# A two-layer decoder trunk: the first norm's sums with tokens on partitions, and a turn counter set to zero before attention

## The chip, the cores and the metric

The kernel runs on one core of one Trainium2 chip. The metric is the device time of one execution in microseconds (us). Three runs of the kernel before took 1446.49, 1443.2 and 1445.98 us; the median is 1445.98 us.

## The reference, cut to what matters

Two layers are computed on 512 tokens with 1024 features, all in float32. Cut to the lines around the change:

```
def rmsnorm(x, w):
    xf = xf * lax.rsqrt(jnp.mean(xf * xf, axis=-1, keepdims=True) + EPS)
    return xf.astype(x.dtype) * w

mod = c_act @ w_ada + b_ada            # sh1, sc1, g1, sh2, sc2, g2
h = rmsnorm(x, norm1_w) * (1 + sc1) + sh1
u = h @ w_in                           # pool, conv, q, k, v, gates
... three mixers; each is projected, gated by a sigmoid, and summed ...
x = x + g1 * (merged @ w_out)
h2 = rmsnorm(x, norm2_w) * (1 + sc2) + sh2
x = x + g2 * ((silu(h2 @ w_gate) * (h2 @ w_up)) @ w_down)
```

For each token the first norm needs one number, the reciprocal root of the mean square over 1024 features. The kernel holds `x` with features on the 128 partitions, as 8 tiles `x[k]` of 128 features by 512 tokens. The sum over features therefore crosses partitions, and that is done by TensorE.

## The kernel before

**Products.** Every float32 operand is split into a high and a low part of a format that TensorE reads in one pass, and a product is three matmuls (`mm3`, line 163): high by high, high by low, low by high. Weights arrive by DMA as `raw` tiles; ScalarE (ACT) makes `whi` (line 399) and VectorE (DVE) makes `wlo` (line 402). For some tiles in the projection `w_in` of layer 0, ACT makes both `whi` and the negated copy (lines 419 and 421) and a transfer that adds, issued by GpSimd's queue, finishes `wlo` (line 423). There are 3 `raw` buffers, and 5 each of `whi` and `wlo`.

**Order.** The program is written out for all engines by Python code. `matmul`, `transpose` and `pin` fix an instruction's place on its engine in program order; the rest is placed on ACT, DVE and the queues by a scheduling layer of the framework. Each engine works its own list strictly in order. Waits between engines are counts of semaphores; the framework derives them from what reads and writes which tile. In a built program `Activation_49`, `DVE_49` and `PE_49` are the counts of finished instructions of those engines.

**PSUM.** TensorE's outputs lie in 4 single tiles `mm` and 2 tiles `pair` of two banks each. One `pair` tile, `scratch` (line 872; `pair_126` in the orders below), holds the statistics of the opening in `scratch[:, 0]` and the warm-up's output in `scratch[:, 1]`. In the first stage of layer 0 it is used again: `pair_b = scratch` (line 941), and `pair_b[:, 0]` is the fourth of the four accumulators of the queries, `q_ps[3]`.

**The opening, lines 872 to 934.**
- Nine small matmuls of ones warm TensorE up, and 8 transposes spread the activated condition `c` over the partitions for ACT to copy into `csil`.
- As the tiles `x[k]` land, DVE and ACT square them (lines 894 and 899) and DVE adds them in pairs (line 901). Four matmuls of ones by such a pair add up over partitions in `scratch[:, 0]` (line 902), so that all partitions hold the sums of all 512 tokens.
- Nineteen matmuls of ones (line 906) keep TensorE busy meanwhile.
- ACT takes the reciprocal root (line 908) and its scaled square (line 909), and DVE does one Newton step in two instructions (lines 913 and 914), all on 128x512 elements, into `norm.rstd`.
- `ada_first` (line 499) makes one column of the scale SC1 or of the shift SH1 by a dot product on DVE (line 479) and one small ACT instruction (line 503 or 506).
- `first_scaled(k)` (line 654, DVE at line 657) multiplies `x[k]`, the scale and `rstd`. `first_hi(k)` (ACT, line 661) and `first_lo(k)` (DVE, line 664) then split the normed tile; ACT line 666 keeps it whole.

**The first stage of layer 0, lines 945 to 972.** For k = 0 to 7 the code writes the scale, shift, `first_scaled`, `first_hi` and `first_lo` of tile k + 2 ahead of the matmuls of tile k. Tiles 0 and 1 are written in the opening. For each k the matmuls are: three for each of `q_ps[0]` to `q_ps[3]`, then three for each of three feature tiles. Afterwards ACT copies the queries out of PSUM (lines 711 and 716, called from line 979) and the next features begin in the tile that `q_ps[0]` held.

**Turns.** `mm3` adds the columns of its output to `clock[0]` (line 168); at every 2048 columns `tick` (line 139) lets the attention's generators take a step, which writes their transposes and score products between the matmuls of the gates. The count runs on from stage to stage. Layer 0's attention begins with it at 0, and layer 1's at 1024, because the pooled projection (line 1198) adds two products of 512 in each layer.

Of the kernel before, what the change touches and what calls it, by code (L numbers as in the profile page):

```python
# [12 lines left out]
F32 = mybir.dt.float32  # L13
# [3 lines left out]
AF = mybir.ActivationFunctionType  # L17
ALU = mybir.AluOpType
# [3 lines left out]
P = 128  # L22
D = 1024
S = 512
L = 2
KT = D // P
# [3 lines left out]
TT = S // P  # L30
# [8 lines left out]
EPS = 1e-6  # L39
# [34 lines left out]

WARM = 9

WARM2 = 19

GATE2 = ([("gate", j) for j in range(6)] + [("attn", 0), ("attn", 1), ("gate", 6), ("gate", 7)]
         + [("attn", j) for j in range(2, 8)])  # L80
# [3 lines left out]
def hybrid_trunk(ctx, tc, xT, ws, ada, cols, pool_w, qk_w, crow, pos, con, out):  # L84
    nc = tc.nc
    V, A, T = nc.vector, nc.scalar, nc.tensor
# [10 lines left out]
    def nm(s):  # L97
        uid[0] += 1
        return f"{s}{uid[0]}"

    def bigt(dt=F32R):
        return big.tile([P, S], dt, tag="big", name=nm("big"))
# [4 lines left out]
    def ps_mm():  # L107
        return psum.tile([P, S], F32, tag="mm", name=nm("mm"), bufs=4)

    def ps_pair():  # L110
        return psum.tile([P, 2, S], F32, tag="pair", name=nm("pair"), bufs=2)
# [4 lines left out]
    def sm(shape, dt=F32, tag="sm", bufs=8):  # L116
        return small.tile(shape, dt, tag=tag, name=nm(tag), bufs=bufs)
# [5 lines left out]
    clock = [0, 0]  # L123
# [30 lines left out]
    def matmul(*a, **k):  # L154
        tc.keep_in_program_order(T.matmul(*a, **k))  # L155

    def pin(ins):
        return tc.keep_in_program_order(ins)

    def transpose(*a):  # L160
        tc.keep_in_program_order(T.transpose(*a))  # L161
# [40 lines left out]
    ident = const.tile([P, P], F32, name="ident")  # L202
# [3 lines left out]
    ones = f32(ones_r)  # L206
# [5 lines left out]
    epst = const.tile([P, 1], F32, name="epst")  # L212
# [32 lines left out]
    class Sums:  # L245
        def __init__(self, l, m, j):
            self.l, self.m, self.j = l, m, j
# [181 lines left out]
    split_after, last_hi = [None], [None]  # L429
# [47 lines left out]
    def ada_dot(aw, l, part, j):  # L477

        return V.scalar_tensor_tensor(aw, aw, 1.0, csil, op0=ALU.mult, op1=ALU.mult,  # L479
                                      accum_out=mod[l][:, part, j:j + 1])  # L480
# [4 lines left out]
    def ada_first_load(j, after=None, parts=(SC1, SH1)):  # L485
        tiles = {}
        for part in parts:
            tiles[part] = w4([P, D])
            with issued_after(after):
                nc.sync.dma_start(tiles[part], ada[0, part, j])  # L490
        return tiles
# [7 lines left out]
    def ada_first(j, tiles, part):  # L499
        first_dots[j, part] = pin(ada_dot(tiles[part], 0, part, j))  # L500
        m = mod[0][:, part, j:j + 1]
        if part == SC1:
            ins = A.activation(amod[0][0][:, j:j + 1], m, AF.Identity, scale=minus[:, j:j + 1],
                               bias=abias[:, j:j + 1])
        else:
            ins = A.activation(m, m, AF.Identity, bias=colt[:, 0, C_ADA + part * KT + j:C_ADA + part * KT + j + 1])
        if j == 0:

            pin(ins)
# [69 lines left out]


    class Norm:
        def __init__(self, one=False):
            self.one = one
            self.low = []
            self.acc = bigt(F32)
            self.last = bigt(F32)
            self.sums = [(bigt(), bigt()) for _ in range(1 if one else 2)]
            self.rstd = bigt(F32)
            self.hi = [bigt() for _ in range(KT)]
            self.lo = [bigt() for _ in range(KT)]  # L590
            self.h = [bigt(F32) for _ in range(KT)]
# [145 lines left out]
    def to_features(l, qk, which, hp):  # L737
        pt = ps_mm()
        for t in range(TT):
            transpose(pt[:, t * P:(t + 1) * P],  # L740
                      qk[t][:, which, 2 * hp:2 * hp + 2, :].rearrange("p h d -> p (h d)"), ident)
        return split_from(pt, scale=colt[:, l, C_QK + which:C_QK + which + 1])
# [110 lines left out]
    def start(gen):  # L853
        n = next(gen, None)
        if n is not None:
            fibers.append([n, gen])

    def attention(l, qk, v, nrq, prq, y_attn):

        for hp in range(PAIRS):  # L860
            q = to_features(l, qk, 0, hp)
            yield 1
            k = to_features(l, qk, 1, hp)
            y = bigt(), bigt()
            y_attn.append(y)
            yield 2
            for n, i in enumerate(ORDER):
                start(unit(hp, i, q, k, v, y, nrq, prq))
                yield GAP[n]


    scratch = ps_pair()
    norm = Norm()

    rows = [ps_mm(), ps_mm()]
    for i in range(WARM):
# [4 lines left out]
        if i == 6:  # L881
            for j in range(KT):
# [6 lines left out]
    pin(V.scalar_tensor_tensor(abias, colt[:, 0, C_ADA + SC1 * KT:C_ADA + (SC1 + 1) * KT], 1.0,  # L889
                               minus, op0=ALU.add, op1=ALU.mult))  # L890
    sq = [bigt(F32) for _ in range(KT)]
    for k in range(KT):
        if k == 0 or (k % 2 == 1 and k < KT - 1):
            step.append(pin(V.tensor_mul(sq[k], x[k], x[k])))
        else:
            if k in (2, 4):
                h = k // 2 - 1
                pin(A.activation(csil[:, h * S:(h + 1) * S], rows[h], AF.Copy))
            pin(A.activation(sq[k], x[k], AF.Square))
        if k % 2 == 1:  # L900
            step.append(pin(V.tensor_add(sq[k], sq[k - 1], sq[k])))
            matmul(scratch[:, 0], ones, sq[k], start=(k == 1), stop=(k == KT - 1))
    first[0].update(ada_first_load(0, step[3], (SH1,)))
    idle = ps_mm()
    for _ in range(WARM2):
        matmul(idle[:, :P], ones, ones, start=True, stop=True)
    y, y2, t = bigt(F32), bigt(F32), bigt(F32)
    A.activation(y, scratch[:, 0], AF.Abs_reciprocal_sqrt, bias=epst, scale=1.0 / D)
    split_after[0] = A.activation(y2, y, AF.Square, scale=(0.5 / D) ** 0.5)
    ada_first(0, first[0], SC1)  # L910
    ada_first(0, first[0], SH1)

    pin(V.scalar_tensor_tensor(t, scratch[:, 0], D * EPS, y2, op0=ALU.add, op1=ALU.mult))
    pin(V.scalar_tensor_tensor(norm.rstd, t, 1.5, y, op0=ALU.subtract, op1=ALU.mult))
    norm.first_scaled(0)
    norm.first_hi(0)
    fetch_after[0] = step[4]
# [19 lines left out]
    for l in range(L):  # L937
# [38 lines left out]
        ss = sm([P, TT, 2, HEADS], tag="ssq", bufs=1)  # L976
# [204 lines left out]
            return sg  # L1181

        m01, y_attn = [], []
        fibers.append([5, attention(l, qk, v, nrq, prq, y_attn)])
        bulk.append((0.4, pool_weights))
        for j in range(2):
# [45 lines left out]
        for step, j in GATE2:  # L1232
# [16 lines left out]
            t = sg2.pop(j)  # L1249
# [73 lines left out]
        norm = n2  # L1323
# [88 lines left out]
        for part, (along, single, pairs) in enumerate(PARTS):  # L1412
# [46 lines left out]
            else:  # L1459
# [7 lines left out]
                scratch = ps_pair()  # L1467
                bank = scratch[:, 1]
                tail(lambda k: act[k], blk, G2, nk, n1, False, lead(n1, l + 1, 0, bank), 4)
                norm = n1  # L1470
# [100 lines left out]
```

## Time and profile before

| what | value |
|---|---|
| runs | 1443.2, 1445.98, 1446.49 us |
| span of the profiled execution, first to last instruction | 1440.7 us |
| time of the profiled execution outside its span | not recorded; the runs' median is 5.3 us above the span |
| TensorE (PE) busy | 1428.3 us, 99% |
| DVE, ACT, GpSimd busy | 1062.3, 750.8, 165.7 us |
| transfers | 251.28 MB |

In the timeline a row gives the start and the time taken by instructions that follow one another, the engine, the line, output and inputs, their number, and in brackets the idle time of the engine before it with what ended that. PE is the matmuls, PEld the loads of weights beside them. Buffer numbers are left out, so `big` stands for many tiles. Line numbers are those of the kernel before. In the list of windows each engine's busy time stands with its number of instructions, and PEclk is the clock granted to TensorE as a share of the full one.

### The profile page before, as it was taken

Reading aid. Unit: us, or ns where it says so; the run is one execution under the profiler, and the core shown is the slowest. Engines: PE = TensorE matmul, PEld = TensorE weight load, DVE = VectorE, ACT = ScalarE, POOL = GpSimd, SP = SyncE. Lnnn points to the kernel's source line nnn. Section 1 sums busy time; section 2 is a strip of 40 time slices with the busy share of each in tenths; the row PEclk is TensorE's granted clock in tenths of the full one; section 3 lists DMA queues with packets and bytes.
Section 4 is the critical chain, followed back from the end, with each engine's and each line's share of the span. In section 5 each row is a group of like instructions: output and inputs, shape, how many; then the busy total and the mean of one; then the engine's idle time right before and its main releaser. Section 6 shows DMA issues by size and latency. Waiting matters only on the chain.

```text
span 1440.7 us, 22089 instructions
## 1 busy us (share of the span) xinstructions
PE 1428.3 (99%) x8298; PEld 1253.2 (87%) x8298; DVE 1062.3 (74%) x1944; ACT 750.8 (52%) x1260; POOL 165.7 (12%) x230
## 2 busy tenths in 40 slices
PE   9999999999999999999999999999999999999999
PEld 7887788887989998989988887888889989989997
DVE  8899767579786867767789986665878747657663
ACT  6776666633554452535454675666336525525450
POOL 0111000101100210211002000011020102111200
PEclk9999999999999999999999999999999999999999
DMA  9877666697446766747528665567773537646532
GB/s 359 234 199 192 175 162 161 159 322 236 119 128 213 196 177 203 191 131 209 195 88 248 170 149 133 133 158 186 253 207 84 141 109 180 172 109 184 138 85 85
DMA packets 94283, 251.28 MB, mean 174 GB/s; under 512 B 11992, under 2 KB 24672, under 8 KB 94176
## 3 DMA queue, kind: packets, MB, share of 16 engines
q1 hardware_dynamic: 67312, 177.37, 36.6%
q0 software_dynamic: 26272, 72.37, 25.3%
q8 instruction: 65, 1.06, 0.3%
q14 instruction: 42, 0.34, 0.1%
q10 hardware_dynamic: 592, 0.14, 0.0%
HBM read 247.73 MB, written 2.10 MB: 173 GB/s over the span
## 4 chain that ended last, share of the span: by engine, by line
PE 86%; DVE 8%; ACT 2%; DMA 2%; issue 1%; ACTq 0%; DVEq 0%; SPq 0%
PE mm L155 75%; PE pair L155 10%; DVE w L479 2%; DVE wlo L402 1%; PE mm L161 1%; DMA raw<-in_ws 1%; DMA wlo<-in_ws 0%; DVE big L676 0%; DMA w<-in_ada 0%; DVE big L1209 0%; DVE big L664 0%; DVE tmp L657 0%; ACT whi L419 0%; ACT big L675 0%; ACT whi L399 0%
## 5 line engine op out<-in xcount | busy, mean ns | idle before, releaser
L155 PE MATMUL mm<-big,whi 128*128 128x512 f32 (+1 forms) x4350 | 1080.4, 340 | 4.2 <-DVE big L676 1.9
L155 PEld LDWEIGHTS mm<-big,whi 128*128 128x128 f32 x4350 | 745.2, 190 | 92.9 <-DVE big L676 2.6
L155 PE MATMUL mm<-big,wlo 128*128 128x512 f32 (+1 forms) x2175 | 736.4, 339 | 0.4 <-DMA wlo<-in_ws 0.4
L155 PEld LDWEIGHTS mm<-big,wlo 128*128 128x128 f32 x2175 | 413.2, 190 | 46.3 <-issue 1.1
L399 ACT ACTIVATE whi<-raw 128x1024 fp32r<-128x1024 f32 (+2 forms) x186 | 191.6, 1031 | 194.1 <-PE mm L155 118.7
L402 DVE TENSOR_TENSOR wlo<-raw,whi 128x1024 fp32r<-128x1024 f32 (+2 forms) x186 | 218.8, 1185 | 41.6 <-ACT whi L399 40.9
L399 ACT ACTIVATE whi<-w 128x1024 fp32r<-128x1024 f32 x84 | 88.9, 1058 | 154.8 <-PE mm L155 94.7
L402 DVE TENSOR_TENSOR wlo<-w,whi 128x1024 fp32r<-128x1024 f32 x84 | 101.2, 1220 | 29.2 <-ACT whi L399 28.5
L1258 DVE SCALAR_TENSOR_TENSOR x<-mm,mod,x 128x512 f32<-128x512 f32 (+1 forms) x89 | 61.5, 693 | 74.1 <-PE mm L155 73.7
L479 DVE SCALAR_TENSOR_TENSOR w<-w,csil 128x1024 f32<-128x1024 f32 x88 | 105.0, 1219 | 13.0 <-DMA w<-in_ada 12.8
L261 POOL DMA_DIRECT2D w<-in_ws x72 | 47.9, 680 | 460.9 <-DVE wlo L402 258.6
L423 POOL DMA_DIRECT2D wlo<-in_ws x50 | 43.0, 861 | 388.1 <-ACT wlo L421 223.7
L263 POOL DMA_DIRECT2D w<-in_ws x72 | 63.9, 903 | 169.9 <-DMA w<-in_ws 162.8
L155 PE MATMUL pair<-whi,big 128*128 128x512 f32 x256 | 83.1, 390 | 0.0
L155 PE MATMUL pair<-big,whi 128*128 128x256 f32 (+1 forms) x376 | 74.0, 294 | 0.0
L419 ACT ACTIVATE whi<-raw 128x1024 fp32r<-128x1024 f32 x50 | 53.1, 1063 | 38.7 <-PE mm L155 28.5
L155 PEld LDWEIGHTS pair<-big,whi 128*128 128x128 f32 x376 | 60.4, 191 | 2.2
L155 PEld LDWEIGHTS pair<-whi,big 128*128 128x128 f32 x256 | 48.1, 188 | 9.9
L675 ACT ACTIVATE big<-big 128x512 fp32r<-128x512 f32 x52 | 32.5, 627 | 45.2 <-DVE big L1251 24.1
L155 PE MATMUL pair<-big,wlo 128*128 128x256 f32 (+1 forms) x188 | 55.4, 295 | 0.0
L421 ACT ACTIVATE wlo<-whi 128x1024 fp32r<-128x1024 f32 x50 | 52.6, 1059 | 0.4
L676 DVE TENSOR_TENSOR big<-tmp,big 128x512 fp32r<-128x512 f32 x48 | 33.0, 691 | 24.2 <-ACT big L675 23.2
(233 smaller groups left out, 1416.0 us busy)
## 6 DMA issues: line engine op xcount, KB each, us to landing
raw<-in_ws SPq DMA_DIRECT2D x146, 512.0 KB, 4.3
w<-in_ada SPq DMA_DIRECT2D x88, 512.0 KB, 5.8
w<-in_ws POOLq DMA_DIRECT2D x144, 256.0 KB, 4.6
wlo<-in_ws POOLq DMA_DIRECT2D x50, 512.0 KB, 6.5
raw<-in_ws SPq DMA_DIRECT2D x64, 256.0 KB, 3.8
raw<-in_ws SPq DMA_DIRECT2D x24, 384.0 KB, 3.3
raw<-in_ws SPq DMA_DIRECT2D x16, 448.0 KB, 6.4
raw<-in_ws SPq DMA_DIRECT2D x36, 128.0 KB, 3.2
```

Source lines behind the costliest of these rows:

```text
L155: tc.keep_in_program_order(T.matmul(*a, **k))
L261: nc.gpsimd.dma_start(dst, self.source(0, 1))
L263: nc.gpsimd.dma_start(dst, self.source(*other), accum_op=ALU.add)
L399: A.activation(hi[:, :n], raw[:, :n], AF.Copy)
L402: ins = V.tensor_sub(lo[:, :n], raw[:, :n], f32(hi)[:, :n])
L419: A.activation(hi[:, :n], raw[:, :n], AF.Copy)
L421: A.activation(lo[:, :n], f32(hi)[:, :n], AF.Copy, scale=-1.0)
L423: nc.gpsimd.dma_start(lo[:, i:i + m].rearrange("p b n -> p (b n)"), src, accum_op=ALU.add)
L479: return V.scalar_tensor_tensor(aw, aw, 1.0, csil, op0=ALU.mult, op1=ALU.mult, accum_out=mod[l][:, part, j:j + 1])
L675: A.activation(hi, src, AF.Copy)
L676: last_split[0] = V.tensor_sub(lo, src, f32(hi))
L1258: V.scalar_tensor_tensor(x[k][:, lo:hi], src, mod[l][:, part, k:k + 1], x[k][:, lo:hi], op0=ALU.mult, op1=ALU.add)
```

## The change

The diff is whole but for unchanged lines.

```
-WARM2 = 19
+WARM2 = (9, 10)
...
     class Norm:
-        def __init__(self, one=False):
+        def __init__(self, one=False, spread=True):
...
-            self.rstd = bigt(F32)
+            self.rstd = bigt(F32) if spread else None
...
-    norm = Norm()
+    norm = Norm(spread=False)
...
     sq = [bigt(F32) for _ in range(KT)]
+    groups = []
+
+    def sum_tokens(t, last):
+        for i in range(TT):
+            matmul(scratch[:, 0, 2 * i:2 * i + 2], t[:, i * P:(i + 1) * P], ones[:, :2],
+                   start=not groups and i == 0, stop=last, skip_group_check=True)
+        groups.append(t)
+
     for k in range(KT):
-        if k == 0 or (k % 2 == 1 and k < KT - 1):
+        if k == 0 or k % 2 == 1:
             step.append(pin(V.tensor_mul(sq[k], x[k], x[k])))
...
-        if k % 2 == 1:
+        if k >= KT - 2:
+            sum_tokens(sq[k], k == KT - 1)
+        elif k % 2 == 1:
             step.append(pin(V.tensor_add(sq[k], sq[k - 1], sq[k])))
-            matmul(scratch[:, 0], ones, sq[k], start=(k == 1), stop=(k == KT - 1))
+            sum_tokens(sq[k], False)
     first[0].update(ada_first_load(0, step[3], (SH1,)))
     idle = ps_mm()
-    for _ in range(WARM2):
+    for _ in range(WARM2[0]):
         matmul(idle[:, :P], ones, ones, start=True, stop=True)
-    y, y2, t = bigt(F32), bigt(F32), bigt(F32)
-    A.activation(y, scratch[:, 0], AF.Abs_reciprocal_sqrt, bias=epst, scale=1.0 / D)
-    split_after[0] = A.activation(y2, y, AF.Square, scale=(0.5 / D) ** 0.5)
+    ss = scratch[:, 0, :2 * TT].rearrange("p (t c) -> p t c", c=2)[:, :, 0]
+    y, t, r = [sm([P, TT], tag="root", bufs=3) for _ in range(3)]
+    split_after[0] = A.activation(y, ss, AF.Abs_reciprocal_sqrt, bias=epst, scale=1.0 / D)
     ada_first(0, first[0], SC1)
+    pin(V.scalar_tensor_tensor(t, ss, D * EPS, y, op0=ALU.add, op1=ALU.mult))
+    pin(V.scalar_tensor_tensor(t, t, 0.5 / D, y, op0=ALU.mult, op1=ALU.mult))
+    pin(V.scalar_tensor_tensor(r, t, 1.5, y, op0=ALU.subtract, op1=ALU.mult))
+    for i in range(TT):
+        transpose(scratch[:, 1, i * P:(i + 1) * P], r[:, i:i + 1].to_broadcast([P, P]), ident)
+    for _ in range(WARM2[1]):
+        matmul(idle[:, :P], ones, ones, start=True, stop=True)
     ada_first(0, first[0], SH1)
-
-    pin(V.scalar_tensor_tensor(t, scratch[:, 0], D * EPS, y2, op0=ALU.add, op1=ALU.mult))
-    pin(V.scalar_tensor_tensor(norm.rstd, t, 1.5, y, op0=ALU.subtract, op1=ALU.mult))
+    norm.rstd = scratch[:, 1]
     norm.first_scaled(0)
...
         m01, y_attn = [], []
+        clock[0] = 0
         fibers.append([5, attention(l, qk, v, nrq, prq, y_attn)])
```

Squares with 128 tokens each are now the stationary operand and two columns of ones the moving one, so that the sums come out with tokens on partitions, in 4 columns of PSUM. The root and the Newton step work on 128x4 elements. Four transposes spread the result over all partitions into `scratch[:, 1]`, and `norm.rstd` is that half of the PSUM tile: `first_scaled` reads it there for all eight k.

TensorE's list at the first products of the opening, with the waits that stand in the built program. Before, `whi_249` is the first weight tile, `big_134` and `big_142` are the high and low part of tile 0, `mm_282`, the two halves of `pair_281`, and `pair_126` (the tile `scratch`) are `q_ps[0]` to `q_ps[3]`:

```order
L155 MATMUL mm_282<-whi_249,big_134 128x512 [waits Activation_49]
L155 MATMUL mm_282<-wlo_251,big_134 128x512 [waits DVE_49]
L155 MATMUL mm_282<-whi_249,big_142 128x512 [waits DVE_49]
...
L155 MATMUL pair_126<-whi_249,big_134 128x512
L155 MATMUL pair_126<-wlo_251,big_134 128x512
L155 MATMUL pair_126<-whi_249,big_142 128x512
L155 MATMUL mm_283<-big_134,whi_249 128x512 [waits PE_49]
```

The same place now, where the names are `whi_267`, `big_133` and `big_141`, and `mm_300` is `q_ps[0]`:

```order
L155 MATMUL mm_227<-ones 128x128 x9
L161 MATMUL pair_126<-ident,root_239 128x128 [waits DVE_49]
L161 MATMUL pair_126<-ident,root_239 128x128 x3
L155 MATMUL mm_227<-ones 128x128 x10
L155 MATMUL mm_300<-whi_267,big_133 128x512 [waits Activation_49]
L155 MATMUL mm_300<-wlo_269,big_133 128x512 [waits DVE_49]
...
L155 MATMUL pair_126<-whi_267,big_133 128x512 [waits DVE_49]
L155 MATMUL pair_126<-wlo_269,big_133 128x512
L155 MATMUL pair_126<-whi_267,big_141 128x512
L155 MATMUL mm_301<-big_133,whi_267 128x512 [waits PE_49]
```

The first matmul into `pair_126` has a wait for DVE that it did not have. In the built program its count is the one that the third row of line 657 reaches, `first_scaled(2)`: the code writes that reading of `scratch[:, 1]` ahead of the first write to `scratch[:, 0]` by `q_ps[3]`, and both are the same tile. In the same way the first `q_ps[3]` matmul of each k up to 5 waits for `first_scaled(k + 2)`, and `first_scaled(k + 3)` waits for the last `q_ps[3]` matmul of k.

ACT's list around the end of that first stage, before. Lines 399 and 419 split weights, lines 711 and 716 empty `q_ps[0]` (`mm_282`):

```order
L399 ACTIVATE whi_551<-raw_549 128x1024 [waits DMAHW6_49,PE_49]
L711 ACTIVATE w_576<-mm_282 128x512 [waits PE_49]
L716 ACTIVATE tmp_604<-mm_282 128x512
L399 ACTIVATE whi_628<-raw_626 128x1024 [waits DMAHW7_49]
L711 ACTIVATE w_577<-pair_281 128x512 [waits PE_49]
```

And now (`mm_300` is `q_ps[0]`):

```order
L399 ACTIVATE whi_569<-raw_567 128x1024 [waits DMAHW6_49,PE_49]
L399 ACTIVATE whi_646<-raw_644 128x1024 [waits DMAHW7_49,PE_49]
L419 ACTIVATE whi_652<-raw_650 128x1024 [waits DMAHW0_49,PE_49]
L711 ACTIVATE w_594<-mm_300 128x512 [waits PE_49]
L716 ACTIVATE tmp_622<-mm_300 128x512
L711 ACTIVATE w_595<-pair_299 128x512 [waits PE_49]
```

Two splits of weights, each of which waits for its transfer, stand ahead of the copies that empty `q_ps[0]`.

TensorE's list in layer 1, in the gate where attention's first four transposes stand, before (`mm_8632` is the gate, three matmuls for each of 8 k):

```order
L155 MATMUL mm_8632<-big_7230,whi_8468 128x512
L155 MATMUL mm_8632<-big_7238,whi_8468 128x512
L155 MATMUL mm_8632<-big_7230,wlo_8470 128x512
L161 MATMUL mm_8645<-ident,w_7954 128x128
L161 MATMUL mm_8645<-ident,w_7955 128x128
```

And now, where `mm_8650` is the same gate:

```order
L155 MATMUL mm_8650<-big_7250,whi_8486 128x512
L155 MATMUL mm_8650<-big_7258,whi_8486 128x512
L155 MATMUL mm_8650<-big_7250,wlo_8488 128x512
L161 MATMUL mm_8669<-ident,w_7972 128x128
L161 MATMUL mm_8669<-ident,w_7973 128x128
```

The transposes stood after the second k of that gate (`big_7230`) and stand after the fourth now (`big_7250`). All of layer 1's attention moves later by such half turns; layer 0's attention keeps its places.

## The prediction

> **What bounds the kernel now.** I read the page's first part, then the list of what TensorE waits for, then the timeline where the change is made.
>
> ```profile
> PE 1428.3 (99%) x8298; PEld 1253.2 (87%) x8298; DVE 1062.3 (74%) x1944; ACT 750.8 (52%) x1260; POOL 165.7 (12%) x230
> ```
>
> ```profile
> PE mm L155 <- DVE big L676: 1.9, 2, 1.7
> PE mm L161 <- DVE big L1209: 1.5, 1, 1.5
> ...
> PE mm L155 <- ACT big L1180: 1.0, 2, 0.5
> ...
> PE mm L155 <- DVE big L1209: 0.6, 1, 0.6
> ...
> PE pair L155 <- DMA wlo<-in_ws: 0.4, 1, 0.4
> ```
>
> TensorE (PE) is busy 99% of the span, and after the opening it seldom waits longer than 0.6 us. So a microsecond that PE loses early is not given back later: behind it stand 1420 us of matmuls, and the other engines are fed by them. What counts is when PE starts its products, and whether it runs on from there. The opening before, where PE, DVE and ACT hand on to one another:
>
> ```profile
> 10.46 0.30 PEld L155 LDWEIGHTS pair<-big,ones 128*128 128x128 f32 x2 [0.66 <-DVE big L901]
> 11.42 4.21 PEld L155 LDWEIGHTS mm<-ones 128*128 128x128 f32 x37 [0.24 <-issue]
> 16.23 0.51 PE L155 MATMUL mm<-whi,big 128*128 128x512 f32 x1 [0.40 <-ACT big L661]
> ...
> 18.59 0.63 PE L155 MATMUL pair<-whi,big 128*128 128x512 f32 x2
> 19.05 0.39 PE L155 MATMUL pair<-wlo,big 128*128 128x512 f32 x1
> ```
>
> ```profile
> 8.76 0.69 DVE L901 TENSOR_TENSOR big<-big,big 128x512 f32<-128x512 f32 x1
> 10.34 1.23 DVE L479 SCALAR_TENSOR_TENSOR w<-w,csil 128x1024 f32<-128x1024 f32 x1
> 13.07 0.69 DVE L913 SCALAR_TENSOR_TENSOR big<-pair,big 128x512 f32<-128x512 f32 x1 [0.21 <-ACT big L909]
> 13.80 0.69 DVE L914 SCALAR_TENSOR_TENSOR big<-big,big 128x512 f32<-128x512 f32 x1
> 14.61 0.75 DVE L657 SCALAR_TENSOR_TENSOR tmp<-x,am,big 128x512 f32<-128x512 f32 x1
> 18.62 0.75 DVE L657 SCALAR_TENSOR_TENSOR tmp<-x,am,big 128x512 f32<-128x512 f32 x1 [0.46 <-ACT am L503]
> 24.60 0.75 DVE L657 SCALAR_TENSOR_TENSOR tmp<-x,am,big 128x512 f32<-128x512 f32 x1
> 29.22 0.74 DVE L657 SCALAR_TENSOR_TENSOR tmp<-x,am,big 128x512 f32<-128x512 f32 x1
> ```
>
> The four rows of line 657 are `first_scaled(0)` to `(3)`. PE makes its first product at 16.23 and then goes on without a gap; its matmuls stand 0.23 apart (18.82, the second of the row at 18.59, and 19.05). `q_ps[3]` of k = 0 begins with that second matmul, at 18.82.
>
> **The change: the wait at `q_ps[3]`.** By the built program (the order in the section on the change) this matmul now waits for `first_scaled(2)`, since that reads the spread root in the tile that `q_ps[3]` writes. Before, `first_scaled(2)` ended at 24.60 + 0.75 = 25.35. Queued behind the waiting matmul are the other 11 of k = 0 and all that follows, so PE, not DVE, bears the wait. The release moves only as `first_scaled(2)` does, and 9.99 us of DVE and ACT work lie between `first_scaled(0)` and it. So first: when does `first_scaled(0)` come now?
>
> *Sums.* There are 20 matmuls of 128x128 by two columns, in float32, two records each. No row has this form. The warm-up's loads are the nearest, 4.21 / 37 = 0.114 each and so 0.23 for two: the loads are the same 128x128, only the columns get fewer. From above I bound it by 0.30 (the two loads at 10.46), from below by an estimated 0.10, if a load hides. I take 0.23. Twelve of them come after the addition that ends at 8.76 + 0.69 = 9.45, which gives 12.2. [...]
>
> *Root and spread.* Small instructions replace those of 0.69 us:
>
> ```profile
> 3.88 0.18 ACT L879 ACTIVATE ccol<-pair 128x8 f32<-128x8 f32 x1 [1.02 <-PE pair L161]
> 4.55 0.17 DVE L889 SCALAR_TENSOR_TENSOR abias<-colt,minus 128x8 f32<-128x8 f32 x1
> 4.70 1.86 PE L161 MATMUL mm<-ident,ccol 128*128 128x128 f32 x8
> ```
>
> One root at 0.18 and three steps at 0.17, with a hand-over of about 0.3 between engines, take 1.3 us. They lie beside the nine warm-ups (9 x 0.23 = 2.1 us), which stand ahead of the transposes on PE: 14.3. Four transposes cost 4 x 1.86 / 8 = 0.9, or half of that where they overlap, and a hand-over 0.3: `first_scaled(0)` at 15.0 to 15.5, say 15.2. That is 0.6 later than 14.61; the two instructions of 0.69 and the squared root that go are eaten by work on PE. The ten warm-ups behind the transposes fill a time in which PE would wait for tile 0 anyway and cost nothing; without that cover they would cost 2.3. DVE's dot for the shift (1.23, as at 10.34) runs during the warm-ups.
>
> *From there to `first_scaled(2)`.* ACT has slack in between:
>
> ```profile
> 16.43 0.95 ACT L399 ACTIVATE whi<-raw 128x896 fp32r<-128x896 f32 x1 [0.26 <-DMA raw<-in_ws]
> 17.29 0.71 ACT L666 ACTIVATE big<-tmp,mod 128x512 f32<-128x512 f32 x1
> 18.20 0.39 ACT L503 ACTIVATE am<-mod,abias,minus 128x1 f32<-128x1 f32 x1 [0.20 <-DVE w L479]
> ```
>
> The gaps 0.26 and 0.20 can take up 0.46 of the 0.6, so `first_scaled(2)` ends 0.1 to 0.6 later than 25.35; I take 25.7. An earlier `first_scaled(0)` would help little: the split at 16.43 waits for its transfer, and lines 666 and 503 follow it. With the sum at 0.10 the release is at 25.1, with 0.30 (+0.8) at 26.4. **The wait costs 25.7 - 18.82 = +6.9 (6.3 to 7.6).** For k = 1 PE comes to `q_ps[3]` after 12 + 9 more matmuls, 25.7 + 21 x 0.23 = 30.5, when `first_scaled(3)` has ended (29.22 + 0.74 + 0.35 = 30.3), so further waits are small at most.
>
> **The clock.** Such a wait leaves PE idle. The trace has one place where idleness cost clock:
>
> ```profile
> 337.00:339.00 2.00, 0.50 (x3) 0.08 (x1) 2.00 (x4) 0.00 (x0) 0.00 (x0) 1.00 0.17 37
> 339.00:341.00 2.00, 1.22 (x3) 0.48 (x3) 1.30 (x4) 1.15 (x2) 0.00 (x0) 0.97 0.96 287
> 341.00:343.00 2.00, 1.77 (x5) 1.47 (x5) 2.00 (x3) 1.84 (x3) 0.00 (x0) 0.50 0.54 205
> 343.00:345.00 2.00, 2.00 (x7) 1.56 (x7) 2.00 (x4) 0.18 (x1) 0.00 (x0) 0.67 0.78 252
> ```
>
> In these windows the first number behind the length is PE's busy time, and the granted clock is the one before the DMA share. PE was busy 0.50 + 1.22 of 4 us, and afterwards the clock was 0.50 for 2 us and 0.67 for 2. That is (0.50 + 0.33) x 2 = 1.7 us of work lost, as much as 3.4 us at half clock. A wait of 6.9 us is emptier than that stretch, so I expect the same once: **+1.8 (0.9 to 3.0)**, 0.9 where half of the slow time falls into the wait itself. The Trainium skill (TensorE: Matmul & The Clock Gate, section "What's actually happening") says that the clock halves after a fully idle window of 3.4 us whose start runs free. The trace agrees on 3.4 us at half, but shows it after a stretch that was only partly idle; by the page 6.9 us hold a whole window at any start, so it gives the same term.
>
> **What PE's lateness hides.** Two waits of before may go:
>
> ```profile
> 22.45 0.19 PEld L155 LDWEIGHTS mm<-whi,big 128*128 128x128 f32 x1 [0.49 <-DVE big L664]
> ```
>
> ```profile
> 80.77 0.47 PE L155 MATMUL pair<-wlo,big 128*128 128x512 f32 x1 [0.38 <-DMA wlo<-in_ws]
> ```
>
> The low part of tile 1 is ready long before 25.7 (-0.2, as a part of the 0.49 lies beside the matmul before it), and the transfer at 80.77, issued ahead, is met later (-0.4). **-0.6.**
>
> **ACT's order at the end of the stage.** Two splits now stand ahead of the copies that empty `q_ps[0]`:
>
> ```profile
> 51.92 0.57 ACT L711 ACTIVATE w<-mm 128x512 f32<-128x512 f32 x1
> 52.39 0.58 ACT L716 ACTIVATE tmp<-mm 128x512 f32<-128x512 f32 x1
> 54.88 1.06 ACT L399 ACTIVATE whi<-raw 128x1024 fp32r<-128x1024 f32 x1 [1.91 <-DMA raw<-in_ws]
> ```
>
> ```profile
> 55.45 0.62 PE L155 MATMUL mm<-big,whi 128*128 128x512 f32 x2
> ```
>
> The first split ends at 55.94, the second at 57.0 or later, the copies 1.15 after that, 58.2; PE came to the emptied tile at 55.45, which would be 2.7 us of waiting. But PE comes 8 us later now (6.9 + 1.8 - 0.6), at 63.5. The splits wait for their transfers and for buffers that PE frees some matmuls earlier, so by then they should be over. I take 0, covered by PE's lateness; without that cover 2.7.
>
> **The counter.** Layer 0 starts at 0 already and stays. In layer 1 the attention's pieces stand 1024 columns later, in the phase that layer 0 has. Of the waits listed above, line 1180's two (1.0) and line 1209's 0.6 are layer 1's and come from the old phase. The row of 1.5 at line 161 is layer 0's, in the phase that layer 1 gets:
>
> ```profile
> 159.22 0.55 PE L161 MATMUL mm<-ident,tmp 128*128 128x128 f32 x3 [1.50 <-DVE big L1209]
> ```
>
> **I take -1.6**; the bounds are -2.7 (the smaller waits of layer 1 go as well) and +1.5 (layer 1 gets such a seam and keeps the others).
>
> **Sum:** 6.9 + 1.8 - 0.6 - 1.6 = +6.5. The profiled span of 1440.7 stands 5.3 below the median with no time of its own, so I count that distance as unchanged: 1445.98 + 6.5 = **1452.5 us**.
>
> **Rivals.**
>
> *The opening's own clock halves too.* Between 7 and 12 us PE now has small matmuls with gaps, some 0.9 us after each addition, where matmuls of 512 columns stood before. That is not far from the 1.72 busy of 4 in the windows above. Then the warm-ups and transposes run at half for up to 3.4 us, `first_scaled(0)` is 1.7 later and with it the release: +8.2, **1454.2**. Against it: no gap there is as long as the one in the windows. 0.26.
>
> *The clock is not lost, or is back before PE restarts.* +6.5 - 1.8 = +4.7, **1450.7**, and 1449.6 if layer 1 gives 2.7. It decides where the low clock falls wholly into the wait. 0.19.
>
> *Not slower: the wait is met when PE arrives.* The opening's chain would have to be so much shorter that `first_scaled(2)` ends by 18.8, 6.6 before 25.35. Then the opening costs 0.4 (its own lateness), ACT's order bites with 2.7, and the counter gives -1.6: +1.5, **1447.5**. The removed work in the chain (0.69 twice, and the wider root) speaks for a gain, but only of that size, and the rows at 16.43 to 18.20 hold it back. 0.05.
>
> **How the numbers follow.** The forecast as summed has 0.48, the rivals 0.26, 0.19 and 0.05; 0.02 is left for a gain that I don't see. A measurement of this kernel tells 0.3% (4.3 us) from no change, so the same lies between 1441.6 and 1450.3. Into it fall the last rival, half of the one before, and 0.05 of the forecast (wait 6.3, clock 0.9, counter -2.7: +3.9, 1449.9): 0.20. Slower: 0.78; faster: 0.02. The range goes from 1448.5, which is below the kept clock with all of the counter's gain (1449.6) by the 1.1 that the wait's sum may be too high (6.9 against 6.3, and the unsure -0.6), to 1457.0: wait 7.6, clock 3.0 and nothing from the counter give +10.0, 1456.0, and a part of the cold opening comes on top.
>
> **What would show it.** In the changed profile PE stops after nine matmuls near 17 us and the first `q_ps[3]` matmul starts near 25.7, released by DVE's line of `first_scaled`; the granted clock drops near 0.5 behind 25 us for some 3 us; layer 1's waits for lines 1180 and 1209 are gone. The prediction is wrong if that matmul starts before 20, if PE waits at `q_ps[3]` for later k too, if the copies out of `q_ps[0]` hold PE near 63, or if layer 1 shows new waits of over 1 us.

## The result and the profile after

The changed kernel took 1452.32 us (median of 4 runs, 1450.66 to 1455.24) beside 1445.89 for the kernel before (4 runs, 1443.2 to 1446.49). The ratio is 1.0057 with a 95% interval of 1.004 to 1.0075, which is 8.2 us (5.8 to 10.8): slower, and inside the forecast range. It is not the quotient of the two medians, which is 1.0044 or 6.4 us and lies in the same interval. The forecast was 1452.5, 6.5 above before. That closeness is partly luck, as the profiles show: their spans are 1440.7 and 1451.3, 10.6 apart and not 6.5. In every run of the changed kernel the time lies 1.8 above the span (1453.09 and 1451.3 in the profiled one), so the profiled run of before took about 1440.7 + 1.8 = 1442.5, some 3.4 below its median, and the profiled run after lies 0.8 above its own.

The list of what PE waits for, after; the first number is the sum in us, then come the number of waits and the longest:

```profile
PE pair L155 <- DVE tmp L657: 6.4, 1, 6.4
PE mm L155 <- DVE big L676: 1.7, 1, 1.7
PE mm L161 <- DVE big L1225: 1.6, 1, 1.6
PE pair L155 <- POOL ones L207: 1.1, 1, 1.1
PE mm L155 <- ACT big L675: 0.6, 1, 0.6
PE mm L155 <- DMA wlo<-in_ws: 0.4, 2, 0.3
```

The first row is new and is the wait at `q_ps[3]`. The row of layer 1's two waits for line 1180 (now 1195) and the 0.6 for line 1209 (now 1225) are gone; layer 0's wait at line 161, which the prediction calls a seam, is still there (1.6). The timeline of PE in the opening after:

```profile
7.69 5.88 PE L155 MATMUL pair<-ones,big 128*128 128x2 f32 x40
13.43 4.19 PE L155 MATMUL mm<-ones 128*128 128x128 f32 x18
17.41 1.00 PE L161 MATMUL pair<-ident,root 128*128 128x128 f32 x4
18.24 2.40 PE L155 MATMUL mm<-ones 128*128 128x128 f32 x20
20.39 0.48 PE L155 MATMUL mm<-whi,big 128*128 128x512 f32 x1
...
22.49 0.39 PE L155 MATMUL pair<-whi,big 128*128 128x512 f32 x1
29.30 0.80 PE L155 MATMUL pair<-whi,big 128*128 128x512 f32 x1 [6.43 <-DVE tmp L657]
```

After the nine matmuls from 20.39 on PE stands still for 6.43 us and restarts at 29.30, where `q_ps[3]` began at 18.82 before: 10.5 later. The same nine warm-ups that were to take 2.1 us took 4.19, and the windows of the opening say why (the last figures are granted clock, DMA share and GB/s):

```profile
8.00:10.00 2.00, 1.93 (x18) 1.84 (x18) 1.90 (x4) 0.63 (x1) 0.00 (x0) 1.00 1.04 418
10.00:12.00 2.00, 2.00 (x18) 2.00 (x17) 1.53 (x3) 0.00 (x0) 0.00 (x0) 0.85 1.03 419
12.00:14.00 2.00, 2.00 (x11) 2.00 (x10) 0.03 (x1) 0.33 (x2) 0.00 (x0) 0.50 1.03 415
14.00:16.00 2.00, 2.00 (x11) 2.00 (x11) 1.60 (x5) 1.35 (x3) 0.00 (x0) 0.50 1.03 408
16.00:18.00 2.00, 2.00 (x11) 2.00 (x11) 0.00 (x0) 0.00 (x0) 0.00 (x0) 0.50 1.02 409
18.00:20.00 2.00, 2.00 (x19) 2.00 (x18) 1.47 (x2) 0.63 (x2) 0.00 (x0) 0.95 1.03 401
```

The clock was at half from about 11.4 to 18.2, although PE's busy time reads 1.93 to 2.00 of every 2 us. `first_scaled(0)` therefore started only at 18.53, and `first_scaled(2)` 9.97 later:

```profile
18.53 0.75 DVE L657 SCALAR_TENSOR_TENSOR tmp<-x,am,pair 128x512 f32<-128x512 f32 x1 [2.86 <-PE pair L161]
...
28.50 0.74 DVE L657 SCALAR_TENSOR_TENSOR tmp<-x,am,pair 128x512 f32<-128x512 f32 x1
```

Behind the wait the clock is at half again, from 25.0 to 35.3:

```profile
24.00:26.00 2.00, 0.00 (x0) 0.00 (x0) 1.89 (x4) 1.50 (x3) 0.00 (x0) 0.76 0.58 174
...
30.00:32.00 2.00, 2.00 (x6) 1.55 (x5) 2.00 (x5) 0.68 (x2) 0.00 (x0) 0.50 0.89 220
32.00:34.00 2.00, 2.00 (x6) 1.58 (x5) 2.00 (x6) 1.48 (x4) 0.00 (x0) 0.50 1.07 324
34.00:36.00 2.00, 2.00 (x7) 1.59 (x7) 2.00 (x3) 1.29 (x2) 0.00 (x0) 0.68 0.99 323
```

Of this, 29.3 to 35.3 falls on work, 6.0 us at half. The matmuls stand about 0.43 apart there instead of 0.23:

```profile
30.32 0.63 PE L155 MATMUL pair<-whi,big 128*128 128x512 f32 x1
30.75 1.05 PE L155 MATMUL mm<-big,whi 128*128 128x512 f32 x2
```

That costs somewhat less than half of the 6.0: PE is 10.48 later than before when it restarts and 13.02 later at the end of the slow stretch, so the low clock cost 2.5.

To see where lateness arises and where it is given back, I paired the matmuls of each profile with those of before, counted from the last one backwards, and took the difference of their starts. The first column is how much later `first_scaled(0)` starts than its 14.61 of before. The next four are PE's lateness at four places by the time of before; the attention of layer 1 lies between the last two. Rows are the changed kernel and the experiments below, by the names that stand there in brackets.

```
kernel         first_scaled(0)  at 63.8   318.8   799.0  1215.4  from 799 to 1215
changed                  +3.92   +12.80  +12.47  +13.76  +10.50             -3.26
counter_only             +0.29    +0.29   +1.26   +1.89   -1.47             -3.36
wide_sums                +0.87    +9.55   +9.68   +8.42   +5.14             -3.28
own_tile                 +4.36    +4.37   +3.44   +3.58   +0.73             -2.85
wide_own                 +1.00    +1.01   +1.06   +1.43   -1.21             -2.64
opening_only             +5.22   +14.00  +14.16  +13.29  +13.53             +0.24
before_shared            +0.45    +7.94   +7.29   +5.78   +6.85             +1.07
short_own                +0.65    +0.89   +3.55   +3.59   +0.59             -3.00
phase_layer0             +0.13    +0.13  +13.65  +13.65  +10.53             -3.12
```

In the changed kernel nearly all loss arises before 64 us, 3.3 comes back in layer 1, and the 1.3 between 318.8 and 799.0 is the clock once more: behind the wait near 340 (1.7 for DVE's line 676) it was at half for 6.8 us, and in the profile of before for 3.4. That one changes sign from kernel to kernel (-1.5 in before_shared).

In counter_only, own_tile, wide_own and phase_layer0 the lateness at 63.8 is that of `first_scaled(0)`, to 0.01. The four kernels in which `q_ps[3]` shares its tile with the root have 7.5 to 8.9 on top of it: the wait and the clock behind it.

### The profile page after: what moved, and what is told of

It reads as the page before. It is cut to its first block, busy times and chain, and to the rows that moved or that the text cites. A ratio compares the mean times of both kernels' runs of the same rounds, so it can differ in the third digit from the quotient of the medians.

```text
span 1451.3 us, 22158 instructions
## 1 busy us (share of the span) xinstructions
PE 1435.0 (99%) x8334; PEld 1263.7 (87%) x8334; DVE 1062.3 (73%) x1945; ACT 750.1 (52%) x1258; POOL 165.7 (11%) x230
## 4 chain that ended last, share of the span: by engine, by line
PE 90%; DVE 4%; DMA 4%; issue 1%; ACT 1%; ACTq 0%; DVEq 0%; POOLq 0%
PE mm L155 77%; PE pair L155 11%; DMA wlo<-in_ws 2%; PE mm L161 1%; DMA raw<-in_ws 1%; DVE w L479 1%; DVE wlo L402 1%; DMA w<-in_ada 0%; DVE raw L479 0%; DVE big L676 0%; DMA colt<-in_cols 0%; DVE big L1225 0%; DVE big L1267 0%; DVE big L902 0%; DVE tmp L657 0%
## 5 line engine op out<-in xcount | busy, mean ns | idle before, releaser
L402 DVE TENSOR_TENSOR wlo<-w,whi 128x1024 fp32r<-128x1024 f32 x84 | 101.2, 1220 | 28.9 <-ACT whi L399 28.2
L155 PE MATMUL pair<-wlo,big 128*128 128x512 f32 x128 | 50.2, 393 | 0.2 <-DMA wlo<-in_ws 0.2
```

The source lines that it names most:

```text
L402: ins = V.tensor_sub(lo[:, :n], raw[:, :n], f32(hi)[:, :n])
```

## The experiments

**The reset alone** (counter_only), in the kernel before:

```
         m01, y_attn = [], []
+        clock[0] = 0
         fibers.append([5, attention(l, qk, v, nrq, prq, y_attn)])
```

> The kernel before with the counter reset alone. In the changed kernel's profile the matmuls of layer 1 lose 3.3 us of their lateness against the profile of before. Theory A, the reset moves layer 1's attention off its waits (lines 1180 and 1209) and does nothing else: 3.3 us faster than before, ratio 0.9977, about 1442.6 us, and the only waits of PE over 0.3 us after 400 us are none. Rival B, those 3.3 us are the lateness of PE itself, which let transfers and DVE get ahead: the reset alone gains 1.6 us or less, and waits for line 1180 or 1209 in layer 1 stay.

Measured: 1440.31 (10 runs) beside 1444.51 (33 runs), ratio 0.9969 (0.9956 to 0.9982). Layer 1 loses 3.36 of its lateness and shows no wait of 0.3 us. So theory A holds: the gain is the phase's, without any help from a late PE. The expected 0.9977 lies inside the interval. This kernel is faster than before and than the changed kernel.

**The opening alone** (opening_only), the changed kernel without the reset:

```
-        clock[0] = 0
```

> The changed kernel without the reset of the counter. Theory A, the two parts add: the opening's loss stays whole (first q_ps[3] matmul near 29.3, clock at half before and behind it), layer 1 has the waits of before for lines 1180 and 1209, and the time is 3.3 us above the changed kernel, about 1455, ratio to before 1.008. Rival B, PE's lateness alone takes layer 1's waits away: the time is within 1 us of the changed kernel's 1452.

Measured: 1457.58 (6 runs) beside 1442.89 (19 runs), ratio 1.0095 (1.008 to 1.0111). From 799 to 1215 it gains nothing (+0.24), although PE is 13 us late, and its list of waits has layer 1's rows of before:

```profile
PE pair L155 <- DVE tmp L657: 6.4, 1, 6.4
...
PE mm L155 <- ACT big L1195: 1.0, 2, 0.5
...
PE mm L155 <- DVE big L1224: 0.6, 1, 0.6
```

Rival B falls: without the reset nothing comes back in layer 1. The distance to the changed kernel is larger than theory A's 3.3 (1.0095 and 1.0057 are 5.5 us apart), and part of that is the opening. Though its program is the same there, its clock was at half from 9.0 to 19.3, so `first_scaled(0)` started at 19.83 and the first `q_ps[3]` matmul at 30.61, not near 29.3.

**The root in a tile of its own** (own_tile). ACT copies the spread root to SBUF:

```
-    norm = Norm(spread=False)
+    norm = Norm()
...
-    norm.rstd = scratch[:, 1]
+    A.activation(norm.rstd, scratch[:, 1], AF.Copy)
```

> The changed kernel, but ACT copies the spread root from PSUM into a tile of SBUF of its own, so that first_scaled no longer reads the tile that q_ps[3] writes. Theory A, the shared tile makes PE wait 6.4 us, and the clock lost behind it is that wait's: first products near 21.1 (20.39 and 0.7 for the copy), no gap at q_ps[3], clock 1.00 from 22 us on. The opening is then 4.9 us late instead of 13.1 and the counter gives back 3.3: 1.6 us above before, 1447.5, ratio 1.001. Rival B, the chain from first_scaled(0) to tile 2 is what is late, and the tile only shows where: PE waits for the parts of tiles 1 and 2 instead, over 3 us in all, and the time is above 1450.

Measured: 1445.78 beside 1444.51, ratio 1.0007 (0.9995 to 1.0019), as theory A said. The rows of PE at `q_ps[3]`:

```profile
22.71 0.39 PE L155 MATMUL pair<-wlo,big 128*128 128x512 f32 x1
22.94 0.62 PE L155 MATMUL pair<-whi,big 128*128 128x512 f32 x2
23.39 0.39 PE L155 MATMUL pair<-wlo,big 128*128 128x512 f32 x1
```

No gap: the second matmul at 22.94 is the first into `q_ps[3]`. In the list of windows of this run the clock is 1.00 in all from 18 to 34 us. The wait and the clock behind it go together, and no wait of over 0.6 us takes their place.

**The sums with 128 columns of ones** (wide_sums) in place of two, otherwise the changed kernel:

```
-            matmul(scratch[:, 0, 2 * i:2 * i + 2], t[:, i * P:(i + 1) * P], ones[:, :2],
+            matmul(scratch[:, 0, i * P:(i + 1) * P], t[:, i * P:(i + 1) * P], ones,
...
-    ss = scratch[:, 0, :2 * TT].rearrange("p (t c) -> p t c", c=2)[:, :, 0]
+    ss = scratch[:, 0].rearrange("p (t c) -> p t c", c=P)[:, :, 0]
```

> The changed kernel with 128 columns of ones in each of the 20 sums in place of two; loads, gaps and instructions stay as they are. Theory A, the clock halves in the opening because a matmul of two columns counts as little work for the clock gate: the granted clock stays 1.00 from 10 to 20 us, first_scaled(0) starts near 15.3 instead of 18.53, the first matmul of q_ps[3] near 25.9 instead of 29.30, and the time falls by about 3.3 us against the changed kernel, to 1449.0 (ratio to before 1.002). Rival B, it halves because of the gaps between the sums: the gaps are the same, the clock is again near 0.50 from 12 to 18 us, and the time stays at 1452.

Measured: 1448.91 beside 1444.51, ratio 1.0025 (1.0015 to 1.0035). Its windows in the opening:

```profile
8.00:10.00 2.00, 1.79 (x17) 1.60 (x15) 1.90 (x4) 0.77 (x2) 0.00 (x0) 1.00 1.05 423
10.00:12.00 2.00, 2.00 (x18) 2.00 (x19) 1.70 (x3) 0.00 (x0) 0.00 (x0) 1.00 1.03 418
12.00:14.00 2.00, 2.00 (x21) 2.00 (x20) 0.67 (x6) 0.99 (x3) 0.00 (x0) 1.00 1.03 411
```

PE is no busier by its records than with two columns (1.79 and 2.00 against 1.93 and 2.00), the gaps are no shorter, and the clock stays at 1.00. So the two columns, not the gaps, halve the clock in the opening. The sums cost hardly more for it:

```profile
9.96 2.94 PE L155 MATMUL pair<-ones,big 128*128 128x128 f32 x24 [0.21 <-DVE big L911]
...
26.26 0.80 PE L155 MATMUL pair<-whi,big 128*128 128x512 f32 x1 [6.43 <-DVE tmp L657]
```

24 records in 2.94 are 0.12 each, 0.24 a sum; with two columns and the clock still full, the first 16 of own_tile took 1.84, or 0.115 each. `first_scaled(0)` starts at 15.48, and PE's gap at `q_ps[3]` is 6.43 as in the changed kernel: in these profiles it does not depend on when the opening ends, since PE's first product and `first_scaled(2)` both follow `first_scaled(0)`.

**Both edits at once** (wide_own).

> Both of these edits at once. Theory A: clock 1.00 throughout the opening, first products near 17.5 (1.3 later than before: sums, transposes and the copy), no gap at q_ps[3], counter -3.3: 2.0 us faster than before, 1443.9, ratio 0.9986. Rival B, the two costs overlap and one of them alone carries the loss: the time is that of the better one of the two single edits, 1447 or more.

Measured: 1442.57 beside 1444.51, ratio 0.9985 (0.9973 to 0.9996). The four combinations lie at 1.0057, 1.0025, 1.0007 and 0.9985: the tile is worth 0.4 to 0.5% and the columns 0.2 to 0.3%, each with and without the other. Neither takes the place of the other. What stays of the new opening is a `first_scaled(0)` at 15.61 instead of 14.61 and a first product at 17.17 instead of 16.23. So the opening is 1.0 slower even without its two costs, and by the table it is the reset (-2.64) that makes this kernel faster than before.

**The shared tile in the kernel before** (before_shared). Sums, root and counter stay; only the place of the root changes:

```
-    pin(V.scalar_tensor_tensor(norm.rstd, t, 1.5, y, op0=ALU.subtract, op1=ALU.mult))
+    pin(V.scalar_tensor_tensor(scratch[:, 1], t, 1.5, y, op0=ALU.subtract, op1=ALU.mult))
+    norm.rstd = scratch[:, 1]
```

> The kernel before with one edit: DVE writes the root into the free half of the PSUM tile (scratch[:, 1]) and first_scaled reads it there; sums, root and counter stay as they were. Theory A, the shared tile is enough for the wait: first products near 16.3, the first q_ps[3] matmul at 25.4 instead of 18.82, a gap of 6.4 us, then the clock at half for 2 to 3 us of work that lost 1 to 1.7 us: about 8.5 us slower than before with no gain behind it, ratio 1.006. Rival B, the wait is bound up with the late opening of the changed kernel: a gap under 2 us, ratio within 1.002.

Measured: 1449.74 (6 runs) beside 1442.89, ratio 1.0044 (1.0029 to 1.0059), 6.3 us; theory A's 8.5 is at the upper end.

```profile
16.68 0.50 PE L155 MATMUL mm<-whi,big 128*128 128x512 f32 x1 [0.41 <-ACT big L661]
...
25.84 0.79 PE L155 MATMUL pair<-whi,big 128*128 128x512 f32 x1 [6.42 <-DVE tmp L657]
```

One instruction's place in memory is enough for the whole wait. The mechanism is settled. The clock behind it cost what theory A had, and less than in the changed kernel, since the slow stretch was shorter:

```profile
22.00:24.00 2.00, 0.00 (x0) 0.00 (x0) 1.92 (x4) 0.66 (x2) 0.00 (x0) 0.51 1.04 415
...
28.00:30.00 2.00, 2.00 (x8) 1.61 (x8) 2.00 (x5) 0.67 (x3) 0.00 (x0) 0.78 0.92 324
```

It was at half from 22.0 to about 28.9, of which 3.0 us fell on work: 1.5 lost. In the changed kernel it was 10.2 us, of which 6.0 fell on work and cost 2.5.

**Fewer warm-ups ahead of the transposes** (short_own), on top of both edits:

```
-WARM2 = (9, 10)
+WARM2 = (2, 17)
```

> The run with 128-column sums and a tile of its own, with two warm-ups ahead of the transposes instead of nine (17 behind them). Theory A, first_scaled(0) sets the pace of the whole first stage, since it and first_scaled(2) lie 10.0 us apart in every profile so far: it starts near 14.6 instead of 15.61 and the time falls by 1.0 us, ratio to before 0.9978. Rival B, the transfer of tile 1's weights and the split behind it set the pace: first_scaled(2) does not move by more than 0.3, and the time stays at 0.9985.

Measured: 1441.52 beside 1442.89, ratio 0.9982 (0.997 to 0.9994). `first_scaled(0)` started at 15.26 and `first_scaled(2)` at 25.25, 0.36 earlier than with both edits alone. Theory A expected 1.0 and rival B at most 0.3, and the intervals hold both: the times decide nothing. The distance of 10.0 held once more. The edit also did something that neither theory named: the 17 warm-ups behind the transposes kept PE from its first product until 18.14, 0.97 later than with both edits alone. Of that little is left at 63.8, where the lateness is 0.89 beside 1.01; `first_scaled(0)` alone, 0.65 later than before, would make it 0.65. So most of a late first product is made up in this stage; a late `first_scaled(0)` is not.

**The other phase in layer 0** (phase_layer0), in the kernel before:

```
+        clock[0] = 1024 * (1 - l)
```

> The kernel before with the counter set to 0 in layer 1 and to 1024 in layer 0, so that layer 0's attention gets the phase that layer 1 had. Theory A, the phase of 1024 columns is what puts the transposes where their inputs are not ready: layer 0 then shows waits for line 1180 of about 0.5 each that it hasn't now and becomes up to 3 us slower than the run with the reset alone, ratio to before about 0.999. Rival B, the wait of 1.4 at line 161 near 160 us belongs to phase 0: it goes, and the time falls below the run with the reset alone, ratio 0.996.

Measured: 1449.62 (8 runs) beside 1442.89, ratio 1.0041 (1.0023 to 1.0059). Both theories missed. The wait at line 161 did go, as rival B said, but larger ones came, and of those that theory A named only one of 0.5:

```profile
PE mm L155 <- DVE w L829: 5.8, 3, 2.6
PE mm L155 <- DMA wlo<-in_ws: 3.5, 1, 3.5
...
PE mm L155 <- ACT big L1180: 0.5, 1, 0.5
```

Line 829 is attention's split of the transposed scores, and PE never waited for it in layer 0 before. Behind two of these waits the clock was at half as well, for 6.8 us from 120.0 and for 3.4 from 219.0. So phase 0 is better than 1024 in layer 0 too, but by other waits than in layer 1. The profiled execution took 1453.02, 3.4 above the median of its kernel, so its list shows more than the usual loss. Why the transfer was 3.5 late, near 121 us, is open; where the other profiles have a wait there, it is 0.1 to 1.3.

**How many columns keep the clock.** Three kernels (cols_16, cols_32 and cols_64), one execution each, with the root in its own tile:

> The run with the root in a tile of its own, with 16 columns of ones in each sum in place of 2 (there the clock halved from 11 to 18 us) or 128 (there it stayed at 1.00). Loads bound all of these at about 0.11 a record. Theory A, what counts for the clock is how many columns pass in a stretch: 16 are an eighth of 128, the clock is at 0.50 for 3.4 or 6.8 us between 9 and 19 us, as with 2. Rival B, anything but the very smallest counts as busy: the clock stays at 1.00.

> The same with 32 columns, a quarter of 128. Theory A: the limit lies between 16 and 64, and this look says on which side 32 is; since PE's first product comes 3 us later with a halved clock (20.6 against 17.2), first products near 20 or near 17. Rival B: clock 1.00.

> The same with 64 columns, a half of 128. Theory A: enough columns pass, the clock stays at 1.00 and the first product is near 17.2. A limit above a half would show the clock at 0.50 here too.

The window from 12 to 14 us with 16, 32 and 64 columns:

```profile
12.00:14.00 2.00, 2.00 (x11) 2.00 (x11) 0.00 (x0) 0.10 (x1) 0.00 (x0) 0.50 1.03 418
```

```profile
12.00:14.00 2.00, 2.00 (x11) 2.00 (x11) 0.00 (x0) 0.00 (x0) 0.00 (x0) 0.50 1.02 415
```

```profile
12.00:14.00 2.00, 2.00 (x20) 2.00 (x20) 1.12 (x4) 1.31 (x3) 0.00 (x0) 1.00 1.03 420
```

PE came to its first product at 20.43, 21.86 and 17.14. Theory A holds: 16 and 32 are too few at this pace, 64 are enough. With 32 the clock was at half for 10.2 us, which is why the first product came after 20. As each was executed once, the limit is between 32 and 64 here and no finer.

## Why the prediction was right and where it was wrong

The likeliest case was not the one that came. The rival "the opening's own clock halves too" (1454.2, chance 0.26) is what happened, though not by its cause: it blamed the gaps between the sums, and wide_sums shows that it was their two columns. Two things the other way brought the total back to the forecast: the counter gave more than forecast, and the profile that the sum was built on was a better one than the median of before.

1. **The wait: mechanism right, 6.9 forecast, 10.5 measured.** PE stopped after nine matmuls and the release was `first_scaled(2)`, in the changed kernel and in the kernel before with nothing else changed; with a tile of its own the wait was gone. The mis-sized term is `first_scaled(0)`: 15.2 forecast, 18.53 measured. With the clock kept it was 15.48 and the restart 26.26, which is +7.4. So the working of sums, root and spread was right to 0.3; the sum's price of 0.23 was 0.24. (The upper bound was added up 0.1 short: 25.7 and 0.8 are 26.5.) The step that failed for the remaining 3.0 is "no gap there is as long as the one in the windows", by which the forecast kept the clock: it looked at gaps, and gaps were not what counted.
2. **ACT's slack of 0.46 took up nothing.** `first_scaled(2)` started 9.97 to 10.0 after `first_scaled(0)` in before, the changed kernel, wide_sums, opening_only, before_shared, wide_own and short_own. That chain is rigid, so each us that `first_scaled(0)` is late reaches all of the first stage. The prediction said that what counts is when PE starts its products; in short_own PE started 1.9 later than before and only 0.89 was left at 63.8.
3. **The cold opening's price.** The rival took one stretch of 3.4 us at half and 1.7; it was 6.8 us (two such stretches) and 3.0 (15.48 to 18.53), and in opening_only 10.2 us and 4.35 (to 19.83).
4. **The clock behind the wait: +1.8 forecast with bounds 0.9 to 3.0, 2.5 measured** in the changed kernel, 1.5 in before_shared. The slow stretch lasted 10.2 us, not the 3.4 that the prediction took over from the other place, but 4.3 of it fell into the wait. The value was too low and the bounds held. The rival by which it is not lost falls in all four profiles with the wait.
5. **What PE's lateness hides: -0.6, right.** At the low part of tile 1 the lateness falls from 13.02 to 12.80, by the 0.2 of the forecast, and stays there to 63.8. Of the 0.38 at 80.77 only 0.23 went, but a second wait for `wlo`, at 116.98 in before, fell from 0.37 to 0.19. The three make 0.64.
6. **ACT's order: 0, right.** The split and the first copy on ACT after:

```profile
63.46 1.06 ACT L419 ACTIVATE whi<-raw 128x1024 fp32r<-128x1024 f32 x1 [3.48 <-PE mm L155]
64.43 0.58 ACT L711 ACTIVATE w<-mm 128x512 f32<-128x512 f32 x1
64.90 0.59 ACT L716 ACTIVATE tmp<-mm 128x512 f32<-128x512 f32 x1
```

The copies end at 65.5, and PE came to the emptied tile at 55.45 + 12.8 = 68.2, without a wait. (The split waited for PE, not for its transfer.)
7. **The counter: -1.6 forecast, -3.3 measured**, beyond the bound of -2.7; the runs put the reset alone at 4.5 us (2.6 to 6.4). The direction and the place were right. I counted the listed waits alone, 1.6 in three rows. A matmul behind such a wait starts 0.66 later than its usual distance where the idle time reads 0.50, and smaller gaps of layer 1 went too; these make up to 2.8, and the last 0.5 I have not traced. A wait like layer 0's at line 161 did not come.
8. **The base.** I left 5.3 between span and median unchanged; 1.8 of it lies outside the span, and the rest is a profile better than the median. The sum against the profile would have had to be 10.6: 3.6 more for the wait, 0.7 more for the clock, 1.7 more gained by the counter, and 1.3 by the clock near 340 make 6.5 + 3.6 + 0.7 - 1.7 + 1.3 = 10.4, near enough. Without the 4.2 by which the two profiles stand differently to their medians, 6.4 is left, the difference of the medians, which the prediction reached by partly wrong terms. That is luck.

The Trainium skill (TensorE: Matmul & The Clock Gate, section "What's actually happening") speaks of an idle window of about 3.4 us ahead of the halving. The length agrees: slow stretches were 6.8 and 10.2 us, two and three times 3.4. The idle window does not: in the changed kernel PE's last matmul ended at 22.88 and the clock fell at 25.0, 2.1 us later. There the measurement decides.

## What to carry to other kernels

A value that was put into the free half of a buffer waited here, and was waited for, with all that the buffer held; before reusing one, look at who writes the other half next and whether the reader comes before it. Beside a busy share of 100% look at the granted clock: a chain of tiny matmuls can be busy and still be slow, and padding them from 2 to 128 columns cost next to nothing here (0.115 and 0.12 us a record). A late start matters where a rigid chain hangs on it: here that was one DVE instruction, not PE's first product. Where a change has two parts, time each alone: here one gained 0.3% and the other lost 1%, and the better kernel was the smaller edit.

## What the runs showed of the hardware

- With matmuls of 128x128 by 2, 16 or 32 float32 columns, 0.11 to 0.14 us a record and PE's records filling 1.5 to 2.0 of every 2 us, the granted clock fell to half; with 64 or 128 columns it stayed at 1.00. That so few columns did not keep the clock is shown; by what measure they count is not.
- The clock fell 2.1 us after PE's last matmul in the changed kernel, 5.2 in wide_sums and 2.6 in before_shared; and it stayed at half for 6.0, 5.5 and 3.0 us of work afterwards, by which PE fell 2.5, 2.5 and 1.5 behind. So the same wait costs 1.5 to 2.5 us by when it comes.
- Within a profile the changes of the clock lie whole multiples of 3.41 us apart (in the changed kernel near 11.4, 18.2, 25.0 and 35.3). In the 3.41 us up to the fall at 25.0 PE was busy for 1.25, and in those up to the fall of before_shared at 22.0 for 0.80. In wide_sums the clock held through such a stretch with 1.67 and fell after the next, which was empty. Where a wait falls on this grid is what differs between these kernels.
- The spread of the runs goes with the clock: of the ten of counter_only the three with a mean clock of 1.000 took 1437.16 to 1438.41, the two with 0.996 and 0.997 took 1441.92 and 1442.35.
